# RWKV key normalization as one factor per token and head: on the triangular matrix and on its solution

## The chip, the cores and the metric

The kernel runs on one core of a Trainium2 chip. The metric is the time of the whole program on the device in microseconds (us), as the median of several runs. The engines are TensorE (PE; its weight loads are listed as PEld), VectorE (DVE), ScalarE (ACT), GpSimd (POOL) and SyncE (SP), whose queue issues most transfers. Each runs its own instructions in program order and waits for the others by semaphores.

## What is computed

Two decoder layers over 1024 tokens of width 1024. The even layer has an RWKV-7 branch (16 heads of 64), an S5 branch and an attention to a memory behind one input projection and one output projection; the odd layer has Mamba-2, latent attention and memory attention. The part that the change touches is the RWKV step:

```python
kk = (k * k_k).reshape(b, s, h, n).astype(jnp.float32)
kk = kk * lax.rsqrt(jnp.maximum(jnp.sum(kk * kk, -1, keepdims=True), 1e-24))
removal = kk * iclr
def step(state, inp):
    r_t, w_t, k_t, v_t, kk_t, b_t = inp              # b_t is removal
    sa = -jnp.einsum('bhij,bhj->bhi', state, kk_t)
    state = (state * w_t[:, :, None, :] + sa[..., None] * b_t[:, :, None, :]
             + v_t[..., None] * k_t[:, :, None, :])
    return state, jnp.einsum('bhij,bhj->bhi', state, r_t)
```

A chunk of 128 tokens is solved at once. With the unnormalized key on one side and the key divided by its squared length on the other, products of pairs of tokens (`ga`) form a triangular matrix that is inverted (`xt`); the inverse times a right side (`rh`) gives `sa` for the chunk's tokens.

## The kernel before

The work of TensorE is written as generators ("streams"), and a small planner, `Flow`, decides in which order they emit their matmuls. It keeps an estimated time, takes the stream of the best rank whose due time has come, and so fixes PE's program order; a `yield` gives a delay after the present planned time, an event, or a number of free PSUM banks (tag `g`). The dense projections (tag `mm`, three fp32r passes for each product of 128x128 by 128x512) are one stream of the worst rank: they fill whatever the others leave. A scheduler then orders the instructions of DVE, ACT, POOL and SP around this order.

The RWKV branch has 16 units: a pair of heads (128 channels) by half of the tokens (512, four chunks of 128). Stream a prepares a unit (`rw_prep0`, lines 569 to 629) and starts the inversion of its 32x32 diagonal blocks on POOL (`rw_inv0`, lines 689 to 717); stream i finishes the inverse with small matmuls (`rw_inv1`); stream b prepares the rest (`rw_prep1`); two streams s run over the chunks (`rw_seq`, lines 770 to 832); stream o normalizes and gates the result (`rw_out`, lines 834 to 863).

In `rw_prep0`, `kh` is the key times `k_k`, `sq` its square. The sum over the 64 channels of a head is a product with the block matrix `blk` of ones: `sq` is split into two fp32r parts (`ce` and `cc`, a cast on ACT at line 404 and a difference on DVE at 405), and two matmuls of 512 columns (`head_sums`) leave each channel's row with its head's sum. DVE takes the maximum with 1e-24 (line 584) and the reciprocal (586) of all 128x512 elements, and POOL multiplies it with `kh` (587); the result `d2` times `ic` (620) and `em` (622) is `bm`, one side of the triangular matrix. Its products with `kr` (`half_products`, printed in the trace as `g<-kr,tg`) are copied out by ACT (653) to `ga`, which goes through memory (`d_in`) into POOL's layout `ai`. POOL's loop of 31 steps, lines 710 and 712, waits for that transfer.

In `rw_seq`, `sp` is the inverse times `rh`, and ACT copies it to `sa` (814). In `rw_out`, DVE forms a mean and a factor per token and head (`gmv`, the last at 877), POOL multiplies (`ty`, line 850), and PE transposes the result (`g<-ident,ty`).

After the RWKV units come the S5 and the memory streams, with the rest of the even input projection and the first output products as filler; then dense work and the odd layer.

Of the kernel before, what the change touches and what calls it, by code (L numbers as in the profile page):

```python
# [10 lines left out]
F32 = mybir.dt.float32  # L11
# [3 lines left out]
A = mybir.AluOpType  # L15
# [4 lines left out]
P = 128  # L20
# [3 lines left out]
HT = 512  # L24
# [100 lines left out]

H = 2.0
HZ = 1.2
HA = 12
HV = 16
S5A = 10  # L130
# [8 lines left out]
BK = 6.5  # L139
# [125 lines left out]
class K:  # L265
# [240 lines left out]
    def rw_consts(self, p):  # L506
        nc = self.nc
        self.m2 = p.tile([P, 2, P], F32, name="m2")
        nc.gpsimd.memset(self.m2, 1.0)
        for i, op in enumerate((A.is_gt, A.is_ge)):  # L510
            nc.gpsimd.affine_select(out=self.m2[:, i, :], in_=self.m2[:, i, :], compare_op=op, fill=0.0,
                                    base=0, pattern=[[1, P]], channel_multiplier=-1)
        self.rst = p.tile([P, P], F32, name="rst")
        nc.vector.memset(self.rst, 1.0)
        nc.vector.memset(self.rst[:, 0:1], 0.0)
        self.p5 = p.tile([P, 1], F32, name="p5")
        nc.vector.memset(self.p5, 0.5)
        self.blk = p.tile([P, P], F32R, name="blk")
        for i in range(2):
            for j in range(2):  # L520
                o = (slice(i * 64, i * 64 + 64), slice(j * 64, j * 64 + 64))
                nc.vector.tensor_scalar(self.blk[o], self.onesD[o], float(D * (i == j)), None, A.mult)

        self.hw0 = p.tile([P, 16], F32, name="hw0")
        o = COFF["rw_w0"]
        nc.vector.tensor_scalar(self.hw0, self.cols[:, o:o + 16], 0.5, None, A.mult)
        self.oka = p.tile([P, 8], F32, name="oka")
        o = COFF["rw_k_a"]
        nc.vector.tensor_scalar(self.oka, self.cols[:, o:o + 8], -1.0, 1.0, A.mult, A.add)

        self.t0 = p.tile([P, 8, 32], F32, name="t0")
        nc.gpsimd.memset(self.t0, 0.0)
        for q in range(4):

            nc.gpsimd.affine_select(out=self.t0[q * 32:(q + 1) * 32], in_=self.t0[q * 32:(q + 1) * 32],
                                    compare_op=A.not_equal, fill=1.0, base=-q,
                                    pattern=[[-4, 8], [1, 32]], channel_multiplier=0)

        self.xts = []
        for i in range(3):  # L540
            xt = p.tile([P, 8, P], F32, name=f"xt{i}")
            nc.gpsimd.memset(xt, 0.0)
            self.xts.append(xt)
        self.xn = p.tile([P, 8, 64], F32, name="xn")
        nc.gpsimd.memset(self.xn, 0.0)
        self.scs = []
        for i in range(4):
            sc = p.tile([P, P], F32, name=f"s0c{i}")
            nc.gpsimd.memset(sc, 0.0)
            self.scs.append(sc)  # L550
# [18 lines left out]
    def rw_prep0(self, st, p, lat, l2, k, wk):  # L569


        nc, F = self.nc, self.flow
        b3 = lambda ap: ap.rearrange("p (b t) -> p b t", b=4)
        l2h, l2l = l2
        kh = self.pp.tile([P, HT], F32, name="tg", bufs=1)
        nc.scalar.mul(kh, k, self.col("rw_k_k", p))
        sq = self.pp.tile([P, HT], F32, name="tb", bufs=1)
        nc.scalar.square(sq, kh)
        parts = self.pp_parts(sq)
        yield [BK, ("g", 1)]  # L580
        ps = self.bank("g")
        self.head_sums(ps, parts)
        d2 = self.pp.tile([P, HT], F32, name="tb", bufs=1)
        nc.vector.tensor_scalar(d2, ps, 1e-24, None, A.max)
        F.rel("g", 2.0)
        nc.vector.reciprocal(d2, d2)
        nc.gpsimd.tensor_tensor(d2, d2, kh, A.mult)
        yield ("g", 2)
        pw, pa = self.bank("g"), self.bank("g")
        for i, o in enumerate((pw, pa)):  # L590
            for j, w in enumerate((l2h, l2l)):
                F.matmul(o, lhsT=w[:, i, :], rhs=lat[:, i], start=(j == 0), stop=(j == 1))
        tw = self.pp.tile([P, HT], F32, name="ta", bufs=1)
        nc.scalar.activation(tw, pw, AF.Tanh, bias=self.hw0[:, p:p + 1], scale=0.5)
        F.rel("g", 2.0)
        F.rel("g", 5.0)
        nc.scalar.activation(tw, tw, AF.Identity, bias=1.0)
        ce = self.pp.tile([P, 4, P + 1], F32, name="ce", bufs=1)
        nc.gpsimd.memset(ce[:, :, 0:1], 0.0)
        for b in range(4):  # L600
            nc.vector.tensor_tensor_scan(ce[:, b, 1:P + 1], self.rst, tw[:, b * P:(b + 1) * P], 0.0,
                                         A.mult, A.add)
        ic = self.pp.tile([P, HT], F32, name="ta", bufs=1)
        nc.scalar.activation(ic, pa, AF.Tanh, bias=self.hw0[:, 8 + p:9 + p], scale=0.5)
        cc = self.pp.tile([P, 4, P + 1], F32, name="cc", bufs=1)
        nc.vector.tensor_tensor(cc, ce, ce[:, :, 64:65].broadcast_to([P, 4, P + 1]), A.subtract)
        fin = wk.tile([P, 12], F32, name="fin", bufs=4)
        nc.scalar.activation(fin[:, 0:4], ce[:, :, 64], AF.Exp, scale=-KDEC)
        e = ce
        nc.scalar.activation(e, cc, AF.Exp, scale=-KDEC)  # L610
        em = cc[:, :, 1:P + 1]
        nc.scalar.activation(em, em, AF.Exp, scale=KDEC)
        nc.gpsimd.tensor_copy(fin[:, 4:8], e[:, :, P])
        nc.gpsimd.tensor_tensor(fin[:, 8:11], fin[:, 4:7], fin[:, 1:4], A.mult)
        nc.scalar.activation(ic, ic, AF.Identity, scale=0.5, bias=self.p5)

        kr = wk.tile([P, 4, 2, P], F32, name="kr", bufs=3)
        nc.vector.tensor_tensor(kr[:, :, 0, :], b3(kh), e[:, :, 0:P], A.mult)

        nc.vector.tensor_tensor(kh, d2, ic, A.mult)  # L620
        bm = b3(kh)
        nc.vector.tensor_tensor(bm, bm, em, A.mult)
        nc.scalar.activation(ic, ic, AF.Identity, scale=self.col("rw_k_a", p), bias=self.oka[:, p:p + 1])
        nc.gpsimd.tensor_tensor(k, ic, k, A.mult)

        ga = wk.tile([P, 4, 2, P], F32, name="ga", bufs=2)
        yield [HA, ("g", 2)]
        self.half_products(bm, kr, 0, ga)
        st.update(fin=fin, kr=kr, ga=ga, e=e, em=em, bm=bm, k2=k)

    def pp_parts(self, x):
# [7 lines left out]
        for i, x in enumerate(parts):  # L639
            self.flow.matmul(ps, lhsT=self.blk, rhs=x, start=(i == 0), stop=(i == 1))  # L640

    def half_products(self, bm, kr, which, out):

        nc = self.nc
        pgs = [self.bank("g", (P, 4, P)) for _ in range(2)]
        for b in range(4):
            for h in range(2):
                hs = slice(h * 64, h * 64 + 64)
                self.flow.matmul(pgs[h][:, b], lhsT=bm[hs, b, :], rhs=kr[hs, b, which], start=True, stop=True)
        for h in range(2):  # L650
            if which == 0:

                nc.scalar.copy(out[:, :, h], pgs[h])
            else:
                nc.vector.tensor_tensor(out[:, :, h], pgs[h], self.m2[:, 1:2].broadcast_to([P, 4, P]), A.mult)
            self.flow.rel("g", 1.5 + 1.2 * h)
# [62 lines left out]
    def rw_inv1(self, st, wk):  # L719
# [19 lines left out]
        F.rel("g", 1.2)  # L739
        yield [HZ, ("g", 1)]  # L740
        zq = self.bank("g", (P, 8, 64))
# [10 lines left out]
        F.rel("g", 1.5)  # L752
        yield [HZ, ("g", 1)]

# [6 lines left out]
        F.rel("g", 1.2)  # L761
        yield [HZ, ("g", 1)]
        zq = self.bank("g", (P, 8, 64))
# [6 lines left out]
    def rw_seq(self, st, s0, i, wk):  # L770

        nc, F = self.nc, self.flow
        fin, kr, tok, gr, km, xt = (st[n] for n in ("fin", "kr", "tok", "gr", "km", "xt"))
        yp = st["yp"] = self.bank("yps", (P, 4, P))
        hsl = [slice(0, 64), slice(64, 128)]
        gbs = [None] * 4
# [13 lines left out]
        for b in range(4):  # L790
# [5 lines left out]
            g = fin[:, 8 + b:9 + b] if b < 3 else fin[:, 7:8]  # L796
# [5 lines left out]
            for h, hs in enumerate(hsl):  # L802
                F.matmul(rp[:, h, :], lhsT=gb[:, h, 0, :], rhs=tok[:, 0, b, hs],
                         start=(h == 0), stop=False)
# [5 lines left out]
            sp = self.bank("g", (P, 2, 64))  # L810
            for h in range(2):
                F.matmul(sp[:, h, :], lhsT=xt[:, 2 * b + h, :], rhs=rh[:, h, :], start=True, stop=True)
            sa = wk.tile([P, 2, 64], F32, name="sa%d" % i, bufs=2)
            nc.scalar.copy(sa, sp)
            F.rel("g", 0.7)
            if b < 3:
                yield ("g", 2)
# [1652 lines left out]
```

## Time and profile before

| | |
|---|---|
| three runs | 2759.63, 2760.64 and 2765.98 us, median 2760.64 |
| profiled execution | 2757.28 us, span 2755.3 us |
| busy over the span | PE 2522.3 us (92%), DVE 1785.2 (65%), ACT 1250.2 (45%), POOL 804.7 (29%) |
| mean granted clock of TensorE | 0.954 of 2.4 GHz |

Busy time says which engine could be the bound. It is an average over stages, so the rows further down take stretches. In "waits", a line names who waited, for whom, the sum in us, how often, and the longest. In the timeline, the bracket at the end of a line is the idle time of that engine before the instruction and what ended it. Start times are in us from the span's start. Matmuls overlap, so the cost of one in a sequence is read from start to start.

### The profile page before, as it was taken

What the parts mean: (1) busy time and instruction counts of PE and PEld (TensorE: products, weight loads), DVE (VectorE), ACT (ScalarE), POOL (GpSimd) and SP (SyncE); (2) the same over time, 40 slices, a digit from 0 to 9 for tenths busy, and PEclk for the clock granted to TensorE, in tenths of its full rate; (3) what the DMA queues carried; (4) which work ended last, traced back from release to release, by engine and by line L of the source; (5) the groups of instructions that cost most, each with busy time, mean ns of one, the idle gap of its engine ahead of it and who ended that gap; (6) DMA issues with size and microseconds to landing.
All of it is one profiled execution on the core that took longest, in us unless ns stands there. A gap on an engine that the chain in (4) does not pass through costs nothing. (4 is left out here: it accounts for less than half of the span.)

```text
span 2755.3 us, 42347 instructions
## 1 busy us (share of the span) xinstructions
PE 2522.3 (92%) x15058; PEld 2036.7 (74%) x15058; DVE 1785.2 (65%) x3366; ACT 1250.2 (45%) x2446; POOL 804.7 (29%) x1507
## 2 busy tenths in 40 slices
PE   7998899999999998888999998988999979998997
PEld 5776677777777776666688776767778768887786
DVE  8756656665755537788656446786743887777532
ACT  7443334443443333545543346435443546655443
POOL 3533554355435403254200111252312020000011
PEclk9999999999999999987999999999999999999999
DMA  4432232333332243355584554142344431113543
GB/s 147 131 100 78 83 94 89 98 89 94 89 100 73 72 133 137 109 151 180 158 280 142 159 183 142 62 108 91 101 144 162 161 117 56 57 50 123 189 133 101
DMA packets 263859, 328.27 MB, mean 119 GB/s; under 512 B 88016, under 2 KB 135248, under 8 KB 263136
## 3 DMA queue, kind: packets, MB, share of 16 engines
q1 hardware_dynamic: 260736, 319.39, 37.6%
q0 software_dynamic: 1280, 4.20, 0.5%
q8 instruction: 119, 1.95, 0.3%
q10 hardware_dynamic: 1632, 1.98, 0.2%
q14 instruction: 92, 0.75, 0.1%
HBM read 232.59 MB, written 92.90 MB: 118 GB/s over the span
## 5 line engine op out<-in xcount | busy, mean ns | idle before, releaser
L405 DVE TENSOR_TENSOR wl<-w,wh 128x512 fp32r<-128x512 f32 (+2 forms) x410 | 287.4, 705 | 282.2 <-ACT wh L404 271.5
L404 ACT CAST wh<-w 128x512 fp32r<-128x512 f32 (+2 forms) x410 | 241.9, 594 | 410.8 <-PE mm L179 259.4
L179 PE MATMUL mm<-xhi,wh 128*128 128x512 f32 x832 | 366.1, 440 | 30.0 <-DVE ev L418 18.5
L179 PE MATMUL mm<-xlo,wh 128*128 128x512 f32 x832 | 341.7, 411 | 4.5 <-DVE xlo L496 2.4
L179 PE MATMUL mm<-xhi,wl 128*128 128x512 f32 x832 | 340.3, 409 | 0.0
L179 PE MATMUL mm<-x1h,wh 128*128 128x512 f32 (+1 forms) x608 | 253.3, 417 | 25.2 <-ACT craw L1818 14.2
L179 PE MATMUL mm<-x1l,wh 128*128 128x512 f32 (+1 forms) x608 | 241.9, 398 | 0.0
L179 PE MATMUL mm<-x1h,wl 128*128 128x512 f32 (+1 forms) x608 | 241.7, 397 | 0.0
L710 POOL TENSOR_TENSOR titmp<-ai,ti 128x60 f32<-128x60 f32 (+24 forms) x496 | 153.1, 309 | 296.5 <-DMA ai<-d_in 259.9
L179 PEld LDWEIGHTS mm<-xhi,wh 128*128 128x128 f32 x832 | 163.9, 197 | 84.6 <-DVE ev L418 20.2
L179 PEld LDWEIGHTS mm<-xhi,wl 128*128 128x128 f32 x832 | 163.8, 197 | 39.7
L179 PEld LDWEIGHTS mm<-xlo,wh 128*128 128x128 f32 x832 | 164.5, 198 | 36.6 <-DVE xlo L474 5.3
L712 POOL TENSOR_TENSOR ti<-ti,titmp 128x60 f32<-128x60 f32 (+24 forms) x496 | 161.3, 325 | 38.2
L179 PEld LDWEIGHTS mm<-x1h,wh 128*128 128x128 f32 (+1 forms) x608 | 117.0, 192 | 59.1 <-ACT craw L1818 17.7
L179 PEld LDWEIGHTS mm<-x1l,wh 128*128 128x128 f32 (+1 forms) x608 | 117.1, 193 | 27.0 <-issue 3.6
L179 PEld LDWEIGHTS mm<-x1h,wl 128*128 128x128 f32 (+1 forms) x608 | 116.6, 192 | 26.8 <-DVE wl L405 0.2
L179 PE MATMUL mm<-yb,wh 128*128 128x512 f32 x320 | 103.6, 405 | 4.3 <-ACT yb L404 4.0
L799 ACT ACTIVATE sn<-s0c,fin 64x64 f32<-64x64 f32 x128 | 44.1, 345 | 104.3 <-DVE s0c L827 57.6
L785 DVE TENSOR_TENSOR gb<-g,m 128x256 f32<-128x256 f32 x128 | 49.4, 417 | 64.3 <-PE g L179 63.8
L1669 POOL TENSOR_TENSOR sq<-sq,sqt 128x512 f32<-128x512 f32 x14 | 18.1, 1289 | 244.9 <-DMA w<-in_w_ev_out 158.8
L418 DVE SCALAR_TENSOR_TENSOR ev<-ev,mm 128x512 f32<-128x512 f32 x72 | 49.0, 681 | 45.5 <-ACT ev L417 45.1
L179 PEld LDWEIGHTS mm<-yb,wh 128*128 128x128 f32 x320 | 61.4, 192 | 20.7 <-ACT yb L404 4.4
(598 smaller groups left out, 6501.7 us busy)
## 6 DMA issues: line engine op xcount, KB each, us to landing
w<-in_w_ev_in SPq DMA_DIRECT2D x106, 256.0 KB
w<-in_w_od_in SPq DMA_DIRECT2D x82, 256.0 KB
w<-in_w_ev_out SPq DMA_DIRECT2D x64, 256.0 KB
w<-in_w_od_out SPq DMA_DIRECT2D x64, 256.0 KB
rd<-ev SPq DMA_DIRECT2D x50, 256.0 KB
spl<-yd SPq DMA_DIRECT2D x40, 256.0 KB
zod<-ev SPq DMA_DIRECT2D x36, 256.0 KB
ai<-d_in SPq DMA_DIRECT2D x16, 512.0 KB
```

The costliest lines, as they stand in the source:

```text
L179: return self._pe(self.nc.tensor.matmul(out, lhsT=lhsT, rhs=rhs, start=start, stop=stop, **kw), math.prod(rhs.shape[1:]), rhs.dtype)
L404: self.nc.scalar.copy(hi, src)
L405: self.nc.vector.tensor_tensor(lo, src, hi.bitcast(F32), A.subtract)
L418: nc.vector.scalar_tensor_tensor(g, g, 1.0, ps, A.add, A.mult)
L710: eng.tensor_tensor(tm, ai[:, s:s + 1, s + 1:32].broadcast_to([P, n, w]), ti[:, 0:n, s:s + 1].broadcast_to([P, n, w]), A.mult)
L712: eng.tensor_tensor(ti[:, 0:n, s + 1:32], ti[:, 0:n, s + 1:32], tm, A.subtract)
L785: nc.vector.tensor_tensor(gb[:, h], pgs[h], self.m2, A.mult)
L799: nc.scalar.mul(sg[hs], sc[hs, hs], g[hs])
L1669: nc.gpsimd.tensor_tensor(self.sq1, self.sq1, t, A.add)
```

## The change

The normalizing factor is no longer applied to the key. It is kept as `kn`, one number per token and head, with the tokens on the partitions: a block of `sq` (128 channels by 128 tokens) becomes the stationary operand of an fp32 matmul whose moving operand is `blk2`, two columns of ones, one for each head. Four such matmuls take the place of the split and the two long ones. The maximum and the reciprocal then run on 128x8 elements. The factor is multiplied into the rows of the triangular matrix when that leaves PSUM (DVE instead of ACT) and into the rows of `sa` (two ACT operations instead of one, each with a scale per partition). POOL's multiplication goes, and the planned delay ahead of the sums is 3 us (`KS`) instead of 6.5 (`BK`).

```diff
+        self.blk2 = p.tile([P, 2], F32, name="blk2")
...
-        parts = self.pp_parts(sq)
-        yield [BK, ("g", 1)]
-        ps = self.bank("g")
-        self.head_sums(ps, parts)
-        d2 = self.pp.tile([P, HT], F32, name="tb", bufs=1)
-        nc.vector.tensor_scalar(d2, ps, 1e-24, None, A.max)
-        F.rel("g", 2.0)
-        nc.vector.reciprocal(d2, d2)
-        nc.gpsimd.tensor_tensor(d2, d2, kh, A.mult)
+        yield [KS, ("g", 1)]
+        ps = self.bank("g")[:, 0:8]
+        for b in range(4):
+            F.matmul(ps[:, 2 * b:2 * b + 2], lhsT=sq[:, b * P:(b + 1) * P], rhs=self.blk2, start=True, stop=True)
+        kn = st["kn"] = wk.tile([P, 4, 2], F32, name="kn", bufs=3)
+        nc.vector.tensor_scalar(kn, ps.rearrange("p (b h) -> p b h", h=2), 1e-24, None, A.max)
+        F.rel("g", 1.0)
+        nc.vector.reciprocal(kn, kn)
...
-        nc.vector.tensor_tensor(kh, d2, ic, A.mult)
+        nc.vector.tensor_tensor(kh, kh, ic, A.mult)
...
-        self.half_products(bm, kr, 0, ga)
+        self.half_products(bm, kr, 0, ga, kn)
...
-                nc.scalar.copy(out[:, :, h], pgs[h])
+                nc.vector.tensor_tensor(out[:, :, h], pgs[h], kn[:, :, h].unsqueeze(2).broadcast_to([P, 4, P]), A.mult)
...
-            nc.scalar.copy(sa, sp)
+            for h in range(2):
+                nc.scalar.mul(sa[:, h], sp[:, h], kn[:, b, h:h + 1])
```

The change also moves instructions, since the planner and the scheduler work from other delays and lengths. On PE, in the sixth unit's preparation, these rows stood in the order before (`lt,l2h` and `lt,l2l` are the first products behind the sums):

```order
L179 MATMUL mm<-xhi,wl 128x512
L179 MATMUL g<-tok,gb_3446 128x64 x2
L179 MATMUL g<-s0c_586,kr 128x128
L179 MATMUL g<-ce,blk 128x512
L179 MATMUL g<-cc,blk 128x512
L179 MATMUL g<-lt,l2h 128x512
L179 MATMUL g<-lt,l2l 128x512
```

And there these stand now:

```order
L180 MATMUL yps<-tok,gb_3351 128x64
L180 MATMUL yps<-sa_3407,gr 128x64
L180 MATMUL g<-blk_549,tb 128x2 x4
L180 MATMUL g<-lt,l2h 128x512
L180 MATMUL g<-lt,l2l 128x512
```

The sums are four short fp32 rows instead of two long ones. They come sooner behind the work of another unit, and over the whole stage 60 dense matmuls (`mm`) that stood ahead of the last RWKV product stand behind it.

On POOL, the fifth unit's `ty` (line 850, now 855) stands inside the inversion loop of the seventh unit. The last number of a row's shape tells the step: 31 in the first, one less in each. Before:

```order
L712 TENSOR_TENSOR ti<-ti,titmp 128x2x25
L710 TENSOR_TENSOR titmp<-ai,ti 128x2x24
L712 TENSOR_TENSOR ti<-ti,titmp 128x2x24
L710 TENSOR_TENSOR titmp<-ai,ti 128x3x23
L850 TENSOR_TENSOR ty<-ty,gmv 128x512
L712 TENSOR_TENSOR ti<-ti,titmp 128x3x23
```

Now:

```order
L716 TENSOR_TENSOR ti<-ti,titmp 128x3x21
L714 TENSOR_TENSOR titmp<-ai,ti 128x3x20
L716 TENSOR_TENSOR ti<-ti,titmp 128x3x20
L714 TENSOR_TENSOR titmp<-ai,ti 128x4x19
L855 TENSOR_TENSOR ty<-ty,gmv 128x512
L716 TENSOR_TENSOR ti<-ti,titmp 128x4x19
```

It moved from the ninth step to the thirteenth. In PE's order 33 dense matmuls stood between the seventh unit's first `kr,tg` product and the fifth unit's transposes of `ty`; now 36 do.

## Rows read from the trace of the kernel before

**Rows 1.** Busy time by stretch: stretch, PE, PEld, DVE, ACT, POOL, clock, DMA share, GB/s.

```profile
40.00:1040.00 1000.00, 929.24 (x6865) 740.53 (x6863) 611.45 (x1340) 400.07 (x838) 434.42 (x1148) 0.95 0.32 94
1040.00:1345.00 305.00, 253.89 (x1630) 205.01 (x1629) 249.97 (x352) 147.94 (x302) 136.52 (x114) 0.88 0.49 146
```

**Rows 2.** PE's waits from 40 to 1040: sum in us, times, longest.

```profile
PE g L183 <- POOL ty L850: 34.5, 13, 6.8
...
PE g L179 <- ACT rh L807: 5.6, 2, 4.3
...
PE g L179 <- DVE tg L622: 3.7, 2, 2.3
```

**Rows 3.** Timeline of one wait for `ty`: start, us, engine, line, operation.

```profile
443.14 0.17 DVE L877 TENSOR_TENSOR gmv<-gmv 128x8 f32<-128x8 f32 x1
...
445.39 0.24 POOL L710 TENSOR_TENSOR titmp<-ai,ti 128x31 f32<-128x31 f32 x1 [18.00 <-DMA ai<-d_in]
...
451.04 1.04 POOL L850 TENSOR_TENSOR ty<-ty,gmv 128x512 f32<-128x512 f32 x1
...
452.14 0.66 PE L183 MATMUL g<-ident,ty 128*128 128x128 f32 x4 [1.90 <-POOL ty L850]
...
454.11 0.63 PE L179 MATMUL mm<-xlo,wh 128*128 128x512 f32 x1
...
454.54 0.63 PE L179 MATMUL mm<-xhi,wl 128*128 128x512 f32 x1
```

**Rows 4.** Timeline, PE: pitch of long matmuls, and of short passes with full weights.

```profile
441.19 0.53 PEld L179 LDWEIGHTS g<-tok,gb 128*128 128x128 f32 x4
...
441.63 0.30 PEld L179 LDWEIGHTS g<-s0c,kr 128*128 128x128 f32 x2
...
443.80 0.40 PE L179 MATMUL g<-ce,blk 128*128 128x512 f32 x1
...
444.03 0.39 PE L179 MATMUL g<-cc,blk 128*128 128x512 f32 x1
```

**Rows 5.** Single operations by line, ns min/median/max; the third from the timeline.

```profile
L586 DVE RECIPROCAL tb<-tb x16: 3341/3353/3354, 78.5 to 904.1; 128x512 f32<-128x512 f32 x16
L584 DVE TENSOR_SCALAR tb<-g x16: 675/691/693, 77.5 to 902.9; 128x512 f32<-128x512 f32 x16
453.63 0.80 DVE L405 TENSOR_TENSOR cc<-tb,ce 128x512 fp32r<-128x512 f32 x1
L587 POOL TENSOR_TENSOR tb<-tb,tg x16: 1270/1284/1726, 81.9 to 910.6; 128x512 f32<-128x512 f32 x16
L653 ACT COPY ga<-g x32: 572/586/599, 92.2 to 924.1; 128x512 f32<-128x512 f32 x32
L655 DVE TENSOR_TENSOR gr<-g,m x32: 673/681/693, 107.5 to 941.8; 128x512 f32<-128x512 f32 x32
L814 ACT COPY sa<-g x64: 242/265/289, 172.0 to 1035.7; 128x128 f32<-128x128 f32 x64
L799 ACT ACTIVATE sn<-s0c,fin x128: 332/344/351, 88.4 to 1028.8; 64x64 f32<-64x64 f32 x128
```

**Rows 6.** What DVE's line 620 waited for: us in total, times.

```profile
  POOL tb L587: 17.3, 7
```

**Rows 7.** Timeline: the copy of `sa` with the least room, and its user.

```profile
913.05 0.25 ACT L814 COPY sa<-g 128x128 f32<-128x128 f32 x1
...
914.42 0.21 PEld L179 LDWEIGHTS g<-sa,tok 128*64 128x64 f32 x4
```

**Rows 8.** Timeline: the square with the least room, and the sums' first matmul.

```profile
105.19 0.63 ACT L578 ACTIVATE tb<-tg 128x512 f32<-128x512 f32 x1
...
114.90 0.40 PE L179 MATMUL g<-ce,blk 128*128 128x512 f32 x1
```

**Rows 9.** S5 and memory stage: PE's largest wait; table loads of line 1213, ns.

```profile
PE mm L179 <- DVE ev L418: 26.4, 5, 8.8
L1213 ACT ACT_TABLE_LOAD  x13: 1283/1283/1283, 89.1 to 1734.3; - x13
```

More of the change, by code (lines that the diff above doesn't have):

```diff
@@ L127 @@
 HZ = 1.2
+KS = 3
 HA = 12
@@ L517, in rw_consts @@
         nc.vector.memset(self.p5, 0.5)
+        self.blk2 = p.tile([P, 2], F32, name="blk2")
+        nc.vector.memset(self.blk2, 0.0)
+        for i in range(2):
+            nc.vector.memset(self.blk2[i * 64:i * 64 + 64, i:i + 1], 1.0)
         self.blk = p.tile([P, P], F32R, name="blk")
@@ L640, in head_sums, with half_products @@
             self.flow.matmul(ps, lhsT=self.blk, rhs=x, start=(i == 0), stop=(i == 1))
-    def half_products(self, bm, kr, which, out):
+    def half_products(self, bm, kr, which, out, kn=None):
         nc = self.nc
@@ L772, in rw_seq @@
         nc, F = self.nc, self.flow
-        fin, kr, tok, gr, km, xt = (st[n] for n in ("fin", "kr", "tok", "gr", "km", "xt"))
+        fin, kr, tok, gr, km, xt, kn = (st[n] for n in ("fin", "kr", "tok", "gr", "km", "xt", "kn"))
         yp = st["yp"] = self.bank("yps", (P, 4, P))
```

## Prediction

> **What bounds the kernel now.** I read the busy time by stretch first, then who PE waits for, then the rows of one such wait. In the RWKV stage (40 to 1040 us) PE is busy 929 of 1000 us, DVE 611, ACT 400 and POOL 434 [rows 1]: PE is the bound, since every gap that the RWKV streams leave is filled with matmuls of the dense stream. So work taken from DVE, ACT or POOL is worth only what it takes out of PE's waits. These are small and have names [rows 2]: 34.5 us in 13 waits for POOL's `ty` (line 850, the last step of a unit's normalization before its transposes), 5.6 us for ACT's `rh`, 3.7 us for DVE's `tg`. After 1040 us comes the S5 and memory stage: PE busy 254 of 305, DVE 250 [rows 1]. There PE waits 26.4 us for the evictions of dense banks that stand behind S5 work on DVE [rows 9].
>
> One wait in full [rows 3]: DVE has the factors `gmv` ready at 443.31; POOL takes up `ty` only at 451.04. In between it stood 18.00 us for the `ai` transfer of another unit's inversion, got it at 445.39, and then ran eight steps and a half of it (5.65 us, 0.66 a step), because its program order has `ty` behind them. PE waits 1.90 us for it. And afterwards matmuls start 0.43 us apart (454.11 and 454.54) instead of 0.23 [rows 4]: TensorE is granted 1.2 instead of 2.4 GHz for a while after such a wait. The stage's mean of 0.95 [rows 1] means about a tenth of it at the lower level. A microsecond of waiting costs half a microsecond more on top.
>
> **Removed and added, engine by engine, for each of the 16 units.** DVE loses a split of 0.80, a maximum of 0.69 and a reciprocal of 3.35 us [rows 5]. It gains the same two on 8 columns, 0.17 each as other 128x8 operations [rows 3], and two evictions of `ga` at 0.68, the price of the same shape for `gr` [rows 5]. Net 4.84 - 1.70 = 3.1 us less, 50 us in all. POOL loses one multiplication of 1.28 us. ACT loses a cast of 0.6, two copies of 0.59 and four of 0.265, and gains eight scaled copies; the nearest row for those is the 64x64 one at 0.344 [rows 5]: 2.8 against 2.75, even. All this lies beside PE. It becomes time only through the waits.
>
> PE: two matmuls of 512 columns, 0.23 each from start to start (443.80 to 444.03), make 0.47. The new sums are four fp32 matmuls, each two passes, each pass with a 128x128 weight load and 2 columns. No row has that form; the nearest are passes with 128x128 weights and 64 columns: four from 441.19 to 441.63, so 0.11 each [rows 4]. Eight make 0.88. So PE pays 0.41 us more a unit, **+6.6 us**. Bounds: 0 if they hide between their neighbours, which no row excludes, and +9 at 0.13 a pass, the 0.53 us that the same four loads were busy; less than nothing is excluded, since eight loads take the place of two.
>
> **Waits that could be added.** (1) The sums come 3 planned us after the unit's start instead of 6.5, so about 3.8 us sooner. Their square must be there: in the tightest row it ends at 105.82 and PE comes at 114.90 [rows 8], 9 us. Cost nothing. (2) `sa` takes two ACT operations instead of one, 0.69 against 0.265, +0.42. The tightest row ends at 913.30 and its user loads at 914.42 [rows 7]: 1.1 us of cover. Cost nothing; were it gone, 64 x 0.42 = 27 us. (3) `ga` moves from ACT to DVE, 0.1 us longer each. Behind it on DVE stand weight splits and transposes for an inversion; it releases the `d_in` transfer and so the inversion. I take it even, since ACT is at times as late as DVE would be.
>
> **Waits that go.** DVE stands 17.3 us, in 7 units, in front of `kh = d2 * ic` for POOL's multiplication [rows 6], and everything behind that stands too. The new product needs no POOL. So the 3.7 us for `tg` go, and most of the one 4.3 us for `rh` [rows 2], since ACT was then standing behind the same chain. **-8 us**; bounds 0 and -11 with the clock.
>
> **Moved.** With its sums sooner, each unit stands a little earlier in PE's order, and after the last RWKV product that order has 2094 dense matmuls behind it instead of 2154. Those 60 (14 us) are not saved; they come later. The order of PE ends the memory stage at 2802 instead of 2796, so the lead is used up by then: it is worth only what it fills of PE's idle 51 us there. That idle time is mostly DVE's, and more dense matmuls bring DVE more splits and evictions. I take **-2 us**, bounds -14 and +10. In that stage ACT's order also has five more table loads, 1.28 us each [rows 9], 6.4 us on an engine busy half the time: no cost on PE, and inside the +10. The Trainium skill, "ScalarE: Activation LUTs", section "What ACT_TABLE_LOAD costs", gives about 2.7 us for a switch with its drain; by that it would be 13.5 us, still on ACT and not on PE, and no row here shows more than 1.28.
>
> On POOL `ty` moves too. For twelve of the fourteen units that have an inversion in front of them it stands 50 steps later in sum (4 steps in the place shown, from the ninth to the thirteenth). At 0.66 to 0.8 a step (the later steps are wider) that is some 34 us later behind the start of the inversion. The inversion starts a fixed way behind PE's `kr,tg` products, and between these and the transposes PE's order now has 90 more dense matmuls (21 us) and some 6 us of small products. So PE comes 27 us later too, and the waits grow by 7. For the other two, one falls by about 4 and one grows by 5: there `ty` moves forward in front of the loop, but PE's transposes move further. In sum **+8 us**, and **+3** for the lower clock behind longer waits. Bounds: -5, if the freed DVE lets the inversion start a microsecond sooner each time; +35, if PE's added work is there already as waits.
>
> **Sum.** 6.6 - 8 - 2 + 8 + 3 = +7.6. The profiled execution took 2757.28, so 2764.9; the median of the three runs lies 3.4 above that execution, so **2768 us**.
>
> **Rivals.** *A, the lead is kept (faster).* If the S5 stage is bound by its own DVE and POOL chain, it ends as much sooner as it begins: 14 us less dense work in front of it, 6.6 more for the sums, 8 to 11 of waits gone, POOL's waits unchanged: -16, 2744 us. For it: DVE is busy 82% there, and PE has 51 us idle. Against: the waits with the longest sums are those of dense banks, not of S5 products, and these come with the added work.
>
> *B, `ty` behind the inversion decides (slower).* If the 34 us of later POOL places meet a PE that is not later (it reaches the transposes by the clock of its waits, not of its work), the waits of [rows 2] double: 6.6 + 30 - 8 = +29 with the clock's share in it, 2789 us. It decides as soon as a step on POOL (0.66 us) is worth more than the dense work put in its place (three matmuls would balance it). For it: 13 of 16 units wait there now, so there is no cover. Against: the place of the `kr,tg` products moves along.
>
> *C, nothing moves.* All that is removed was hidden under a PE that is busy anyway, and the sums cost nothing as their loads hide behind the matmuls in front: within 3 us of 2760. For it: DVE at 61%. Against: 4.3 us waits that do have DVE's name.
>
> **How the numbers follow.** Forecast 0.42, its own range 2758 to 2779; A 0.25; B 0.20; C 0.13. About 0.3% (8.3 us: below 2752.4, above 2768.9) is what a measurement can tell from no change. Faster: nearly all of A, 0.24. Slower: B and not quite half of the forecast, 0.38. Same: the rest, 0.38. Range: A's 2744 and B's 2789 with a little cut from either: 2744 to 2787.
>
> **What would show it.** Right: PE busy in the RWKV stage falls by about 7 us (60 matmuls less, the sums more), DVE's by some 50, and the row PE <- POOL `ty` stays the largest and rises to 40 or 45 us, while those for `tg` and `rh` shrink; the new sums start 0.11 us apart. Wrong: `ty`'s row falling below 30 (then the inversion starts sooner than I think, and A is near), or above 60 (B); PE waiting for `sa`, or for the square; an S5 stage shorter by over 10 us from the last RWKV product to the first `glu` matmul.

## The result: slower by 49 us, in two stages

The changed kernel takes 2814.41 us (median of four runs, 2808.66 to 2818.71); the kernel before, beside it on the same chip, 2763.31. The ratio is 1.0176 with an interval of 1.0153 to 1.0200, so 42 to 55 us slower. The forecast of 2768 and its range up to 2787 were too low. The profiled execution has a span of 2806.9 us against 2755.3; as times they are 2808.66 and 2757.28, some 6 us below either median, so the stages of the two can be laid side by side.

Busy time by stretch of the kernel after, the two lines that answer [rows 1]; columns: stretch, PE, PEld, DVE, ACT, POOL, clock, DMA share, GB/s:

```profile
40.00:1040.00 1000.00, 915.37 (x6800) 730.40 (x6799) 555.52 (x1345) 382.98 (x838) 407.95 (x1132) 0.94 0.30 92
1040.00:1345.00 305.00, 242.35 (x1522) 200.75 (x1521) 216.08 (x297) 131.94 (x256) 115.86 (x102) 0.83 0.44 134
```

DVE is busy 56 us less in the first stretch, POOL 26, ACT 17. PE too, 14, since it gets through less in the same time. The clock of the second stretch is 0.83 instead of 0.88.

Where the stages end is read from PE's timeline, first of the kernel before, then of the one after; columns: start, us, engine, line, operation, and in the bracket the wait before it. The second of the pair `yps<-sa,gr` is the last RWKV product, `mm<-yh,wh` the first output product, `g<-mk,mq` the first score of the memory branch, `mm<-gh,wh` the first `glu` product.

```profile
1039.75 0.39 PE L179 MATMUL yps<-sa,gr 128*128 128x64 f32 x2
...
1250.88 0.79 PE L179 MATMUL mm<-yh,wh 128*128 128x512 f32 x1
...
1264.59 0.79 PE L179 MATMUL g<-mk,mq 64*128 64x256 f32 x1
...
1435.68 0.39 PE L179 MATMUL mm<-gh,wh 128*128 128x512 f32 x1
```

```profile
1056.66 0.39 PE L180 MATMUL yps<-sa,gr 128*128 128x64 f32 x2
...
1291.55 0.51 PE L180 MATMUL mm<-yh,wh 128*128 128x512 f32 x1 [1.73 <-DVE ev L419]
...
1316.43 0.76 PE L180 MATMUL g<-mk,mq 64*128 64x256 f32 x1 [3.14 <-DMA mq<-qd]
...
1488.65 0.40 PE L180 MATMUL mm<-gh,wh 128*128 128x512 f32 x1
```

The RWKV stage ends 16.9 us later, although 60 dense matmuls (14 us) less stand in front of its end. The S5 and memory stage behind it takes 431.9 us instead of 395.8, 36.1 more, of which those 60 matmuls explain 14. Of the 36.1, 35 lie ahead of the first memory score (259.7 instead of 224.7 us behind the last RWKV product): 24 ahead of the first output product, 11 from there to the score. From the score to the `glu` it is 172 and 171. Behind the first `glu` product the two kernels are alike.

Who PE waits for from 40 to 1040 us after the change, the lines that answer [rows 2] (sum, times, longest):

```profile
PE g L184 <- POOL ty L855: 44.1, 13, 8.2
PE g L180 <- DVE xn L731: 9.2, 6, 5.5
PE g L180 <- DVE s0c L832: 7.3, 1, 7.3
PE g L180 <- DVE blk L522: 7.0, 1, 7.0
PE mm L180 <- DVE ev L570: 5.9, 1, 5.9
PE g L180 <- ACT rh L811: 3.3, 1, 3.3
```

The row for `tg` is gone, `rh` fell from 5.6 to 3.3, `ty` rose from 34.5 to 44.1. New are single waits of 6 to 7 us in the first units, at 73 us (`blk`), 135 (`ev`) and 216 (`s0c`). In the second stage (1057 to 1489 us) PE's largest waits are now these; [rows 9] had 26.4 for the first, and none for `yh` above 0.8 or for line 1049:

```profile
PE mm L180 <- DVE ev L419: 27.7, 5, 10.8
PE mm L180 <- ACT yh L405: 10.1, 3, 5.8
PE mm L180 <- ACT ev L1049: 7.6, 1, 7.6
PE g L184 <- DVE rn L1354: 7.4, 1, 7.4
PE g L180 <- ACT mpt L1177: 5.5, 3, 2.5
```

The new operations themselves, by line (ns min/median/max), and the new sums in PE's timeline:

```profile
L819 ACT ACTIVATE sa<-g,kn x128: 291/307/331, 167.7 to 1052.8; 128x64 f32<-128x64 f32 x128
L657 DVE TENSOR_TENSOR ga<-g,kn x32: 669/681/692, 98.3 to 938.9; 128x512 f32<-128x512 f32 x32
L590 DVE TENSOR_SCALAR kn<-g x16: 153/166/168, 75.2 to 920.8; 128x8 f32<-128x8 f32 x16
L592 DVE RECIPROCAL kn<-kn x16: 189/203/204, 75.6 to 921.0; 128x8 f32<-128x8 f32 x16
```

```profile
161.42 0.95 PE L180 MATMUL g<-blk,tb 128*128 128x2 f32 x8
162.23 0.48 PE L180 MATMUL g<-lt,l2h 128*128 128x512 f32 x1
```

Each is priced as forecast: 0.307 for a part of `sa` (0.344 taken), 0.681 for `ga` (0.68), 0.17 and 0.20 for `kn` (0.17 each), and the eight passes of the sums last 0.81 us up to the next product in the place shown (0.88 taken); in the other units it is 0.81 to 0.92, and 1.70 in the first one. So no added operation costs noticeably more than was forecast, and the 49 us are elsewhere.

### The profile page after: what moved, and what is told of

Its sections match the earlier page's. It is cut to its first block, busy times and chain, and to the rows that moved or that the text cites. A ratio compares the mean times of both kernels' runs of the same rounds, so it can differ in the third digit from the quotient of the medians.

```text
span 2806.9 us, 42531 instructions
## 1 busy us (share of the span) xinstructions
PE 2547.8 (91%) x15154; PEld 2055.5 (73%) x15154; DVE 1728.4 (62%) x3385; ACT 1246.7 (44%) x2467; POOL 773.7 (28%) x1491
## 5 line engine op out<-in xcount | busy, mean ns | idle before, releaser
L180 PE MATMUL mm<-x1h,wh 128*128 128x512 f32 (+1 forms) x608 | 254.0, 418 | 26.4 <-ACT craw L1823 16.6
```

The source lines that it names most:

```text
L180: return self._pe(self.nc.tensor.matmul(out, lhsT=lhsT, rhs=rhs, start=start, stop=stop, **kw), math.prod(rhs.shape[1:]), rhs.dtype)
```

## The experiments

Two things changed at once: the operations, and the order that the planner made of the shorter delay and the shorter sums. The first theory was that the order costs the time; its rival, that the operations do. The table has every run; "RWKV end" is the start of the last RWKV product in the profiled execution, "S5, memory" the time from there to the first `glu` product. "Delays" are those ahead of the sums and ahead of the `kr,tg` products: 6.5 and 12 before, 3 and 12 after.

| kernel | ratio to before | interval | RWKV end | S5, memory |
|---|---|---|---|---|
| before | 1 | | 1039.9 | 395.8 |
| after | 1.0176 | 1.0153 to 1.0200 | 1056.8 | 431.9 |
| e1 new operations, old order | 0.9987 | 0.9963 to 1.0012 | 1047.4 | 396.8 |
| e2 old operations, new order | 1.0121 | 1.0091 to 1.0151 | 1058.5 | 425.6 |
| e3 after, `blk2` early | 1.0168 | 1.0139 to 1.0198 | 1078.8 | 428.9 |
| e4 after, `ty` on DVE | 1.0069 | 1.0041 to 1.0097 | 1037.0 | 431.9 |
| e5 delays 3 and 15.5 | 1.0149 | 1.0126 to 1.0172 | 1076.1 | 416.2 |
| e6 delays 6.5 and 8.5 | 1.0109 | 1.0085 to 1.0134 | 1060.3 | 423.0 |
| e7 delays 9.5 and 12 | 1.0105 | 1.0078 to 1.0132 | 1086.9 | 403.3 |
| e8 e1, `ty` on DVE | 0.9938 | 0.9916 to 0.9960 | 1037.3 | 395.2 |
| e9 after, 60 matmuls between the stages | 1.0127 | 1.0105 to 1.0149 | 1070.6 | 418.2 |
| e10 before, `ty` on DVE | 0.9940 | 0.9916 to 0.9964 | 1039.1 | 395.1 |
| e11 before, delay 7 | 1.0141 | 1.0121 to 1.0161 | 1084.4 | 411.9 |
| e12 e9 and e4 | 1.0003 | 0.9989 to 1.0016 | 1044.7 | 415.9 |
| e13 before, 62 dense matmuls out | 1.0016 | 0.9986 to 1.0046 | 1065.7 | 398.9 |
| e14 before, 228 dense matmuls out | 0.9936 | 0.9916 to 0.9956 | 1043.1 | 395.2 |
| e15 before, delay 6 | 1.0074 | 1.0049 to 1.0098 | 1065.3 | 408.1 |
| e16 after, waits for `ty` filled | 1.0201 | 1.0159 to 1.0243 | 1068.5 | 430.7 |
| e17 before, waits for `ty` filled | 1.0093 | 1.0055 to 1.0131 | 1078.4 | 397.6 |

0.1% is 2.8 us. A profiled execution is one of several: e3 has PE's order of the kernel after, and ends the stage 22 us later in its profile while its ratio is the same; the kernel before took 2757 us in its profiled execution, and 2763 to 2776 as median beside the others. So RWKV ends that lie within some 20 us of each other say little. The last column is steadier, and the ratios are what verdicts rest on.

### Operations or order: e1 and e2

e1, in the changed kernel:

```diff
-        yield [KS, ("g", 1)]
+        yield [BK, ("g", 1)]
...
+        F.now += 2 * HT / 2400 - 0.12
...
-        F.rel("g", 1.0)
+        F.rel("g", 2.0)
```

> The changed operations in PE's old order: the delay ahead of the sums is 6.5 again, and the planner is told that the four short matmuls take as long (0.43) and hold their bank as long (2.0) as the two long ones did. PE's order is then that of the kernel before, row by row, but for the sums themselves. Theory 'order' (the 50 us come from the order that the planner made of the shorter sums and the shorter delay, the operations are worth -1 to +7 by the terms 6.6 and -8): 2757 to 2770 us. Rival 'operations' (eviction of ga on DVE, two operations for sa on ACT, fp32 sums cost it): 2800 to 2815. If both count, in between.

e2, in the kernel before:

```diff
-        yield [BK, ("g", 1)]
+        yield [3, ("g", 1)]
...
+        F.now -= 2 * HT / 2400 - 0.12
...
-        F.rel("g", 2.0)
+        F.rel("g", 1.0)
```

> The operations of the kernel before in the new order: delay 3 ahead of the sums, and the planner is told that the two long matmuls take 0.12 and hold their bank 1.0. PE's order is then that of the changed kernel, row by row, but for the sums. Theory 'order': 2795 to 2825 us (the 50 us are there, perhaps a little more, since the split of the square is 3.8 planned us nearer to its matmul). Rival 'operations': 2757 to 2772.

e1 gave -4 us (-10 to +3), e2 +33 (25 to 42). The new operations in the old order are no slower than the old ones; the old operations in the new order lose most of what the change loses. e1's stages end 8 and 9 us behind those of the kernel before, within the spread:

```profile
1047.28 0.39 PE L180 MATMUL yps<-sa,gr 128*128 128x64 f32 x2
...
1444.19 0.39 PE L180 MATMUL mm<-gh,wh 128*128 128x512 f32 x1
```

So the order is the cause: it costs 33 us with the operations of before and 52 with the new ones. Alone the two make some +30 us, together +49; the rest of some 20 (the three intervals together leave 6 to 31) appears only where both are.

### A wait that was no cost: e3

```diff
         nc.vector.memset(self.onesD, 1.0 / D)
+        self.blk2 = c.tile([P, 2], F32, name="blk2")
...
-        self.blk2 = p.tile([P, 2], F32, name="blk2")
...
```

> The changed kernel with the two columns of ones (blk2) written among the first constants instead of with the RWKV constants. In the changed kernel PE's first sums wait 6.99 us for the last of these writes, and 10.2 us at half clock follow (5.1 lost). If that wait is a cost of its own: -7 to -12, so 2802 to 2808 us, and no PE wait for blk2. If PE only waits for the next thing in its place, or DVE's chain behind it is what counts: 2811 to 2818.

The 7.0 us for `blk` are gone from PE's waits, and the ratio is 1.0168 against 1.0176: nothing came of it. At 73.49 us, about where PE stood for `blk`, it now stands for another operand of the first unit (40 to 1040 us):

```profile
PE g L180 <- DVE lt L953: 6.8, 1, 6.8
```

### `ty` off POOL: e4, e8, e10

In the changed kernel, in e1 and in the kernel before:

```diff
-        nc.gpsimd.tensor_tensor(y, y, b8(mv[:, 1]), A.mult)
+        nc.vector.tensor_tensor(y, y, b8(mv[:, 1]), A.mult)
```

> The changed kernel with the multiplication ty (line 855) on DVE instead of POOL, PE's order unchanged. My rival B said that ty behind the inversion on POOL decides. If the 44.1 us of PE's waits for it are real time, they go, and the half clock behind them too (at half a microsecond for each): -45 to -60, 2755 to 2770 us. If PE then waits as long for the next thing (the inverse, the memory stage's DVE), under -15: 2800 or more.

> The kernel of e1 (changed operations, PE's old order) with the multiplication ty on DVE instead of POOL. In e1 PE waits 29.6 us for ty, and at the old order's places some half clock follows each wait. If that is real time as it was in the new order (there -34 us for 44 us of waits): -20 to -30, 2735 to 2750 us. If other waits take its place (the rows for rh and xn grew when it was taken out in the new order): 2755 to 2768.

> The kernel before with the multiplication ty on DVE instead of POOL, nothing else; PE's order unchanged. With the changed operations in this order (e8) that gave a ratio of 0.9938 to before. If the changed operations are worth nothing measurable: ratio 0.992 to 0.998, 2745 to 2765 us. If they are worth more once POOL's ty is out of the way (DVE has 50 us less to do in them and now has ty to do as well): 0.999 or more.

e4 takes 1.07% off the changed kernel (30 us), less than the 45 hoped for. PE's waits in e4 show who takes the place of `ty` (40 to 1040 us):

```profile
PE g L180 <- DVE xn L731: 20.0, 13, 5.9
PE g L180 <- ACT rh L811: 15.5, 5, 9.4
```

9.2 became 20.0 and 3.3 became 15.5: of 44.1 us removed, 23 came back at once. In the old order the same edit is worth 0.5 to 0.6% (14 us in e8 over e1, 17 in e10 over before). So the waits for `ty` cost some 15 us more in the new order than in the old; by the intervals that is uncertain by 12 to 14 us, so barely clear of the noise. e8 and e10 are 0.6% below the kernel before, and level with each other: with `ty` out of the way, too, the changed operations are worth nothing that shows.

With `ty` on DVE on both sides, the change in its new order still costs 36 us (e4 1.0069, e10 0.9940). The profiles, e4 first, put all of it in the S5 and memory stage: 431.9 us against 395.1, while the RWKV stage ends at 1037 and 1039.

```profile
1036.93 0.39 PE L180 MATMUL yps<-sa,gr 128*128 128x64 f32 x2
...
1468.98 0.40 PE L180 MATMUL mm<-gh,wh 128*128 128x512 f32 x1
```

```profile
1039.01 0.39 PE L179 MATMUL yps<-sa,gr 128*128 128x64 f32 x2
...
1434.24 0.39 PE L179 MATMUL mm<-gh,wh 128*128 128x512 f32 x1
```

### Is it the lead, or the place of the sums: e5, e6, e7

The second theory was that what costs is the dense work no longer in front of the last RWKV product (2094 matmuls instead of 2154). e5 has HA (the delay ahead of the `kr,tg` products) at 15.5 instead of 12, e6 has KS 6.5 and HA 8.5, e7 KS 9.5.

```diff
-KS = 3
-HA = 12
+KS = 6.5
+HA = 8.5
```

> The changed kernel with its short delay ahead of the sums (3), but 3.5 more ahead of the kr,tg products (HA 15.5 for 12), so that only the sums themselves come sooner. PE's order then has 2196 dense matmuls ahead of the last RWKV product (the changed kernel 2094, before 2154). Theory 'lead' (what costs is the dense work taken from ahead of the last RWKV product: the RWKV stage does not get shorter by it, and the memory branch waits for the end of the input projection): 2730 to 2768 us. Rival 'place of the sums' (the sums stand too early in PE's order, in front of work that others wait for): 2800 to 2820.

> The changed kernel with the old delay ahead of the sums (6.5) and 3.5 less ahead of the kr,tg products (HA 8.5). The sums come as late as before, all that follows as early as in the changed kernel or earlier; 2055 dense matmuls stand ahead of the last RWKV product. Theory 'lead': slower than the changed kernel, by 0.8 us for each of the 39 fewer matmuls if the slope from 2154 to 2094 holds: 2825 to 2855 us. Rival 'place of the sums': 2757 to 2775.

> The changed kernel with a delay of 9.5 instead of 3 ahead of the sums; 2274 dense matmuls ahead of the last RWKV product. Theory 'lead': if the RWKV stage still has waits that the 120 more matmuls (28 us) fill, and the memory branch starts that much sooner, faster than before: 2700 to 2750 us. If the waits are filled by 2154 already and the longer delay only lengthens each unit's chain: 2760 to 2790.

Both theories fall as the one cause. With 2196 and 2274 matmuls in front instead of 2094 the kernel is 1.0149 and 1.0105, with 2055 it is 1.0109: no slope at all, and e6, with its sums as late as before, is slow too. The edit shown is e6's. In the profiles the RWKV stage is longer with more dense work in front (1076, 1087) and not shorter with less (1060); given the spread above, that is a hint only.

### The S5 stage by its order alone: e9 and e12

```diff
         F.run(self.rw_streams(cp, wk, rd, zr))
+        F.run([F.add(self.wait_for(12.6), 0)])
```

> The changed kernel with 12.6 planned us of dense work alone between the RWKV stage and the S5 stage: 60 dense matmuls (13.8 us) are put there, and from there to the first glu product PE's order is then row for row that of the kernel before. The RWKV stage keeps the new order. Theory 'two stages': the S5 and memory stage loses its 20 us by the place of its products among the dense work, so behind the 60 matmuls it takes the 396 us of before instead of 432 with them inside: -18 to -24, 2788 to 2800 us. Rival 'the RWKV stage alone' (the S5 stage is long since it starts with other data late): 2808 to 2822.

> e9 and e4 together: the changed kernel in the new RWKV order, with the 60 dense matmuls put between the stages and ty on DVE. If the 49 us of the change are the S5 stage's order (20) and the waits for ty with their clock (34 when it was taken out alone): 2755 to 2770 us, level with before. If the two overlap: 2775 to 2790.

e9's stage takes 418.2 us with the 60 matmuls (13.8) in it, 13.7 less than after. So of the 36.1 us, 13.8 are the matmuls, 13.7 the place of S5's and the memory branch's products among the dense ones (uncertain by some 6, the spread of the column for one order), and 8.6 stay: the first S5 transposes (`g<-ident,rn`) come at 64.2 us behind the last RWKV product, where 44.3 and 13.8 would be 58.1, 6.1 less, so S5's preparation does not run ahead under the matmuls. The column "S5, memory" says the same by itself: the seven kernels in the old order of that stage take 395.1 to 398.9 us, the five with the changed kernel's order (after, e2, e3, e4, e16) 425.6 to 431.9, the others, in six more orders of it, 403 to 423. Together with `ty` on DVE (e12) the loss against the kernel before is gone: 1.0003. Against the kernel before with the same edit (e10) 0.6% is left, 17 us.

### Half a microsecond: e11 and e15

```diff
-BK = 6.5
+BK = 7
```

> The kernel before with the delay ahead of its sums at 7 instead of 6.5, half a planned us; 2178 dense matmuls ahead of the last RWKV product instead of 2154, and 93 places of PE's order differ. Theory 'the constants fit one order' (every other order that the planner makes costs waits of its own in both stages): 15 to 40 us slower, 2780 to 2810. Rival 'only delays off by microseconds cost': within 8 us of before.

> The kernel before with the delay ahead of its sums at 6 instead of 6.5. Unlike the half microsecond more (e11), this leaves PE's order as it was but for the sums themselves, which stand one dense product (three matmuls) sooner in each of the 16 units; 2151 dense matmuls stand ahead of the last RWKV product. If what costs is the new order of everything else, as e1 and e2 say: within 6 us of before, ratio 0.998 to 1.002. If any departure from the fitted delay costs: ratio 1.005 or more.

The kernel before, none of its operations changed, loses 39 us with 7 and 20 us with 6. What e15's expectation says of its order was wrong: it differs in 16 places, but three lie in the first RWKV units and 13 in the S5 and memory stage. Yet its RWKV stage is 25 us longer by the profiles (which lie 36 us apart as a whole, where the ratio makes it 20). In it PE waits (40 to 1040 us) for

```profile
PE g L183 <- POOL ty L850: 32.0, 10, 7.5
PE g L179 <- ACT rh L807: 12.7, 4, 8.3
...
PE g L179 <- DVE tg L622: 9.5, 3, 5.9
```

where [rows 2] had 34.5, 5.6 and 3.7. PE's order there is nearly the same; what differs is the orders of the other engines, which the scheduler makes anew (DVE's instructions stand differently in 197 places up to 1300 us). That these make the waits is likely, and not shown. The waits are the smaller part: all of PE's waits from 40 to 1040 us sum to 75 us instead of 71, but PE is at half clock for 150 us instead of 92, and its mean clock there is 0.92 instead of 0.95:

```profile
40.00:1040.00 1000.00, 924.76 (x6708) 736.36 (x6707) 605.81 (x1322) 395.34 (x824) 434.59 (x1146) 0.92 0.31 91
```

### Does less dense work shorten the RWKV stage: e13 and e14

In the kernel before; every third second pass in e14:

```diff
+                            if j == 1 and self.thin:
+                                self.cut += 1
+                                if self.cut % 11 == 0:
+                                    F.now += HT / 2400
+                                    continue
...
```

> The kernel before with every eleventh second pass (xlo,wh) of the dense products left out while the RWKV streams run: 62 dense matmuls less (14 us at 0.23) ahead of the last RWKV product, nothing else in PE's order moved, since the planner counts their time as if they were there; splits, evictions and weight loads from memory stay. A part of the input projection's product is left out by that. Theory 'PE sets the RWKV stage' (my prediction's: the work taken out is saved): -12 to -18 us with the clock, ratio 0.9935 to 0.9957. Theory 'the chain sets it' (the gaps between the units' products grow by what is taken out, and the half clock behind them too): -4 to +6, ratio 0.9985 to 1.002.

> As e13, with every third second pass left out: 228 dense matmuls less (52 us at 0.23) ahead of the last RWKV product. A larger part of the input projection's product is left out. 'PE sets the stage': -45 to -60 us, ratio 0.978 to 0.984. 'The chain sets it': -15 to +10, ratio 0.9945 to 1.004.

62 matmuls (14 us) less: +4 us (-4 to +13). 228 matmuls (52 us) less: -18 (-12 to -23). So 14 us taken out of PE's work in that stage are worth nothing, and of 52 a third. The busy time of e14 from 40 to 1040 us shows where they went:

```profile
40.00:1040.00 1000.00, 923.04 (x6611) 734.56 (x6610) 613.38 (x1335) 400.77 (x837) 434.93 (x1149) 0.89 0.32 94
```

Against [rows 1] PE has 254 matmuls fewer there and is busy 6 us less; its clock is 0.89 instead of 0.95. This execution has one of the two lowest clocks of e14's ten, but the others tell the same: over whole executions on that chip the mean granted clock is 0.949 in the kernel before (20 of them), 0.943 in e13 and 0.938 in e14 (10 each). As an estimate from these, the differences times 2770 us, the lower clock takes back 14 us in e13 and 30 in e14. That leaves 0 of the 14 us taken out and 22 of the 52, where +4 and -18 were measured. So what was taken out came back mostly as time at the lower clock; this fits a clock that sets the price as well as a chain that sets the stage.

### Is that lower clock the price: e16 and e17

In the changed kernel and in the kernel before, ahead of the transposes of `ty` (160 matmuls in all, 37 us at 0.23):

```diff
+        for _ in range(10):
+            F.tc.keep_in_program_order(nc.tensor.matmul(tp.rearrange("p b t -> p (b t)"), lhsT=self.blk,
+                                                        rhs=self.xhi[:, 0, 0:HT], start=True, stop=True))
...
```

> The changed kernel with ten matmuls of 512 columns (2.3 us at 0.23) put ahead of each unit's transposes of ty; they wait for nothing and their result is overwritten by the transposes. They fill up to 2.3 us of each of the 13 waits for ty (27 of 44 us by the list of the waits) and cost 10 us where the wait is shorter. Behind these waits stand 61 us at half clock (31 lost). Theory 'half clock is the carrier' (the waits themselves are slack of the chain, what they cost is the half clock behind them): -10 to -20, ratio to before 1.010 to 1.014. Theory 'chain' (a wait costs its length and the clock only changes who waits): 0 to +10, ratio 1.0165 to 1.021.

> The same ten matmuls in the kernel before. They fill 21 us of its 34.5 us of waits for ty, cost 15.5 us where there is no such wait, and 38 us at half clock stand behind these waits (19 lost). 'Half clock is the carrier': -5 to +5, ratio 0.998 to 1.002. 'Chain': +8 to +16, ratio 1.003 to 1.006.

e16 from 40 to 1040 us, and what is left there of the waits for `ty`:

```profile
40.00:1040.00 1000.00, 922.74 (x6875) 736.32 (x6873) 553.21 (x1338) 379.90 (x830) 406.84 (x1128) 0.95 0.31 90
```

```profile
PE g L184 <- POOL ty L855: 28.4, 8, 6.4
```

The clock is back at 0.95 and `ty`'s waits fell by 16, but the kernel is not faster: 1.0201 against 1.0176. In the kernel before, the same matmuls cost 26 us of their 37 (e17), more than either theory gave. So filling the waits is no gain here.

Whether the half clock is a price of its own these two runs do not settle. Of the 37 us that e16 adds, PE's waits took 7 (all of them together fell from 84 to 77 us) and the higher clock some 15 (96 us at half clock instead of 126); the rest, some 15, is about what its stage grew by (12 us in the profile). For a price speaks e3: PE's order is that of the kernel after and its waits are 88 us against 84, but it is at half clock for 171 us instead of 126, which loses 22 us, and its RWKV stage is 22 us longer. Its stretch from 40 to 1040 us:

```profile
40.00:1040.00 1000.00, 911.36 (x6674) 726.86 (x6673) 543.70 (x1319) 378.89 (x825) 406.57 (x1129) 0.91 0.30 87
```

It shows the two together, and not which of them makes the other.

## Why the prediction was wrong, step by step

**Right: the prices of the operations.** 6.6 for the sums and -8 for the waits that go were -1.4; e1 measured -4 (-10 to +3). In the kernel after the `tg` row went and `rh` shrank, the sums' passes take 0.10 to 0.11 us each, DVE lost 56 us (50 said). That -8 is right by itself is not shown, and the match of the sum is luck in part: in e1 the `tg` row is gone, but these two take its place, against 5.6 and nothing in [rows 2]:

```profile
PE g L180 <- ACT rh L812: 9.4, 2, 5.9
PE g L184 <- POOL ce L605: 7.0, 3, 4.5
```

The steps put at no cost held: PE waits for `sa` once, 1.0 us, and for no square.

**Right in size, small in weight: `ty` on POOL.** The row was to rise to 40 or 45 us and is at 44.1. By e4, e8 and e10 this costs some 15 us more than in the old order (uncertain by some 13), where the sum had 8 + 3. In the place shown in [rows 3], `ty` now runs from 467.01, 4.4 us behind its factors, and PE waits 1.00 instead of 1.90: there PE did come later, as argued.

**Wrong: the term "Moved", -2 with bounds -14 and +10.** It said that the 60 matmuls leave the RWKV stage shorter by their 14 us and lengthen the next by as much, less a little. For all that the order does, the sum had -2 + 8 + 3 = +9; e2 measured +33 (25 to 42). Both halves of the term failed. Taking 14 us of dense work out of the RWKV stage does not shorten it, and taking out 52 shortens it by 18 (e13, e14), while matmuls added in front of `ty`'s transposes lengthen it (e17: 37 us for 26). I called PE the bound by its busy share of 93%, and took its work for time; but busy time holds time at half clock, and what was taken out came back there. I had read [rows 4] as a price of half a microsecond on every microsecond of waiting (by [rows 1] it would be 0.7: 50 us lost on 71 us of idle time); there is no such fixed price, since in e14 the half clock more than doubled with nearly the same waits. And in the S5 stage I looked for where the order ends (2802 instead of 2796 matmuls) and not at what moved inside it: the memory branch can begin only when the dense stream has reached the first output product, which comes 24 us later behind the last RWKV product, 10 more than the matmuls' own 14; and the first score comes another 11 later than that.

**Wrong: the range.** Its upper end, 2787, was rival B alone. B's mechanism was there with about half its price; the S5 stage's +22 had no rival. No term stood for the fact that a new order changes waits all over, of which e11 and e15 give a measure: half a planned microsecond, 20 to 39 us. Seven orders other than the old one were run (after, e2 and e3 share one; e5, e6, e7, e9, e11, e15): each is slower than before, by 0.7 to 1.8%, and only with `ty` on DVE does one come level.

**What stays open.** What the new order's loss in the RWKV stage consists of. With `ty` on DVE it is gone from the profiles (e4, e10), which points to the waits for `ty`; but the sums of PE's waits do not show how: e15's are 4 us more than those of before at 20 us more time. And whether the time at half clock makes a stage longer or follows from a chain that is longer: e3, e13, e14 and e15 fit the first, and no run holds the clock fixed to tell. Nor is it shown why both operations and order together lose some 20 us more than the two apart.

## What to carry to other kernels

When a change shifts a planner's delays or lengths, run the new operations in the old order (give the planner the old lengths) before judging them: here that parts +49 us into -4 for the operations and +33 for the order. That an engine was busy 93% of a stage did not mean here that less work for it is less time, its clock being below full; take a little of its work out and see whether the stage gets shorter. And a filler stream that also feeds a later branch is on that branch's path: count what of it stands ahead of the branch's first instruction, not only ahead of the stage's end.

## What the runs showed of the hardware

With less dense work TensorE was longer at half clock. Over whole executions on one chip its mean granted clock is 0.949 in the kernel before, 0.943 with 62 dense matmuls fewer (e13) and 0.938 with 228 fewer (e14). One place where it can be seen: in the kernel before PE waits 2.30 us for `xn`, and then a stretch of 6.8 us has the granted clock 0.50, the next 13.3 us 1.00 (columns as for the stretches above):

```profile
252.18 0.22 PE L179 MATMUL g<-xn,ga 32*32 32x32 f32 x2 [2.30 <-DVE xn L727]
```

```profile
254.94:261.75 6.81, 6.81 (x67) 5.29 (x66) 3.40 (x7) 3.02 (x8) 2.33 (x3) 0.50 0.10 39
261.80:275.10 13.30, 13.30 (x111) 11.03 (x111) 9.95 (x31) 5.63 (x12) 0.11 (x1) 1.00 0.41 124
```

In e14, at the same products, after 2.77 us:

```profile
249.84 0.22 PE L179 MATMUL g<-xn,ga 32*32 32x32 f32 x2 [2.77 <-DVE xn L733]
```

```profile
251.22:275.10 23.88, 23.88 (x171) 19.37 (x165) 11.65 (x25) 8.85 (x19) 2.83 (x4) 0.50 0.22 67
```

It stays at 0.50 (1.2 GHz) for 23.9 us. PE is busy in all of it, so no list of waits shows this. From 75 to 1035 us, e14's profile has 212 us at half clock where the kernel before has 89, with nearly the same waits (74 and 68 us). The Trainium skill, "TensorE: Matmul & The Clock Gate", section "A second HAM failure mode: psum-queue depth-cycling", tells of a kernel in which short idle times between groups of matmuls make the clock go back and forth, and puts the lost throughput down to that. The first half agrees with these rows. Whether the second holds here is open: by the estimate above the lower clock takes back about what e13 and e14 fail to gain, but e16, which lifted the clock of the RWKV stage from 0.94 to 0.95 with matmuls of its own, was not faster (1.0201 against 1.0176).
